# Weight forms cut in halves, bank copies with priority, single banks for the last two value products, and a later up unit, in a hybrid recurrent/retention block

## The chip, the cores and the metric

The kernel runs on one core of a Trainium2 chip. The core has five engines that work side by side, each through its own instructions in a fixed order: TensorE (PE, with its weight loads as PEld), VectorE (DVE), ScalarE (ACT), GpSimd (POOL) and SyncE (SP), beside 16 DMA engines. Matrix products land in PSUM, eight banks of 128 partitions by 2 KiB. An instruction that waits holds back all that stands behind it on its own engine. The metric is the device time of one execution in microseconds (us); the median of three runs before is 1076.57 us, from 1075.84 to 1076.70.

## The reference, cut to what matters

One block on 512 tokens (and 16 meta tokens ahead of them) of width 1024, all in f32:

```
z = rms_norm(h, norm_mix_g) @ w_in
u_rnn, u_gate, q, k, v, g_ret, ga, gb = split(z)
o_a = rg_lru(conv(u_rnn)) * gelu(u_gate)
o   = retention(rotary(q), rotary(k), v)          # 4 heads, 512 value columns each
o_b = head_rms(o) * silu(g_ret)
mixed = sigmoid(ga) * (o_a @ w_branch_rnn) + sigmoid(gb) * (o_b @ w_branch_ret)
h = h + mixed @ w_out
up = conv(rms_norm(h, norm_ffn_g) @ w_up);  gate, val = split(up)
h = h + (gelu(gate) * val) @ w_down
out = rms_norm(h, norm_final_g)[16:]
```

## The kernel before, in words

Every f32 operand of a product is cut into two fp16 forms: a high one, which ACT writes as a scaled copy (L91), and a low one, the rest, which DVE writes from the source and the high form (L92, `split`). A product is three matmuls (high by high, low by high, high by low). Weights come by DMA into tiles named `raw`, and their forms are written into tiles named `wt`, ten of them in a ring.

Twenty products of the middle of the kernel (the silu gate of retention, eight units; the two sigmoid gates, four and four; and the output of retention into the branch, four, of two weight units each) go by a scheme with seven products of half matrices in place of eight (`fast_products`, L835). Each of the seven is 12 matmuls of 257 columns for one weight unit. Its weight units (`fast_steps`, L234) are made in five steps: two cuts, a step `sums` with three additions on DVE (L253 to L255), two more cuts; a cut is a `split` of 128x512 or 128x1024. The seven products use three PSUM banks, `pa`, `pe` and `pb`. The first product (B11 by A11) goes into `pa` and ACT copies it to `kept` (L848, `keep`); the second (T3 by F7) goes into `pe`; the third (T2 by F6) is added onto `pa`, so it can't begin until that copy is done; it is copied to the other half of `kept`; the fourth goes into `pb`; the fifth (T1 by F5) is again added onto `pa` and copied to `last`; the sixth is added onto `pa` and the gate function `func` reads the bank (L881, names `g<-pa`); the seventh is added onto `pe`. Three DVE additions (L865, L869, L876) join copies and banks.

`gated(h)` (L983) runs the two gate units of a head, and between their products the retention output of the next head (`retention_out`, L928), which hands its tiles `or` on. `ob_forms` (L960) makes the forms `ob` of the gated output on DVE and ACT. `values(h)` (L883) computes the values of a head in five blocks of rows: four full ones (L906) and a small one (L898), each split into forms `v`. Up to here all five take space from PSUM tiles of two banks each (pool `acc`, two such tiles from head 2 on, beside four single banks in pool `bank`); blocks 0 and 1 share one tile, and 2 and 3 the other.

After the mix come the output projection of four row groups (L1179), each followed by an RMS norm: ACT squares and sums (L341) and takes the root (L343), DVE the reciprocal (L345) and the scaling into `xo` (L351), PE transposes (L358) and ACT and DVE split the result into `x2h` and `x2l`. While the last norm runs, PE works on three early half products of the up projection (L406), of which the third needs the second weight unit of `w_up`.

The order on every engine is not written out here: a scheduler places each instruction by the order of the code and by priorities, and `tc.high_priority()` raises one. `get(u)` makes the missing forms of a weight unit at its place in the code, and `tick()` makes one step of the next unit ahead of its use, as far as a bound on tiles allows (`ahead`).

Of the kernel before, what the change touches and what calls it, by code (L numbers as in the profile page):

```python
# [10 lines left out]
AF = mybir.ActivationFunctionType  # L11
ORDERED = {mybir.EngineType.PE, mybir.EngineType.Activation, mybir.EngineType.DVE}
ALU = mybir.AluOpType

P = 128
# [3 lines left out]
D = 1024  # L19
# [31 lines left out]
def hybrid_block_kernel(ctx, tc, x, meta, norm_mix_g, w_in, conv_w, conv_b, rg_a_w, rg_a_b,  # L51
# [21 lines left out]
    def acc(name):  # L73
        return psum["acc"].tile([P, 2, 512], F32, name=name, tag="acc")
# [15 lines left out]
    def split(hi, lo, src, s):  # L90
        nc.scalar.activation(hi, src, AF.Copy, scale=s)  # L91
        nc.vector.scalar_tensor_tensor(lo, src, s, hi, op0=ALU.mult, op1=ALU.subtract)  # L92
# [141 lines left out]
    def fast_steps(rv, bk, bc):  # L234


        tiles = []
        top, low = slice(0, bk), slice(bk, 2 * bk)
        left, right = slice(0, bc), slice(bc, 2 * bc)

        def cut(rows, cols):
            def run():
                t = wsp.tile([P, 2, 1024], F16, name="wt")
                src = rv[:, rows, cols]
                n = bk * src.shape[2]
                tv = [t[:, a, :n].rearrange("p (k c) -> p k c", k=bk) for a in range(2)]
                tiles.append(tv)
                split(tv[0], tv[1], src, SW)
            return run

        def sums():
            pair = rv[:, top].rearrange("p k (h c) -> p h k c", h=2)
            nc.vector.tensor_tensor(pair, pair, rv[:, :, right].rearrange("p (h k) c -> p h k c", h=2), op=ALU.add)  # L253
            nc.vector.tensor_tensor(rv[:, low, right], rv[:, top, left], rv[:, low, right], op=ALU.add)
            nc.vector.tensor_tensor(rv[:, low, left], rv[:, low, left], rv[:, low, right], op=ALU.add)  # L255

        at = {"B11": (0, 0), "B21": (1, 0), "B22": (1, bc), "T1": (2, 0), "T3": (2, bc), "T4": (3, 0), "T2": (3, bc)}

        def form(nm, a, k):
            i, c0 = at[nm]  # L260
            return tiles[i][a][:, k, c0:c0 + bc]

        wviews.append(form)
        return [cut(top, left), cut(low, slice(0, 2 * bc)), sums,
                cut(top, slice(0, 2 * bc)), cut(low, slice(0, 2 * bc))]
# [19 lines left out]
    def get(u):  # L285
        current[0] = max(current[0], u)
        while len(loaded) <= u:
            queue(unit_load())
        while done[0] < len(steps) and steps[done[0]][0] <= u:
            emit_step()  # L290
        return wviews[u]
# [46 lines left out]
    def rms_scale(src, rows, name):  # L338
        junk = work.tile([P, D], F16, name="junk", tag="w")
        ss = small.tile([P, 1], F32, name="ss")  # L340
        nc.scalar.activation(junk[:rows], src, AF.Square, accum_out=ss[:rows])  # L341
        sd = small.tile([P, 1], F32, name="sd")
        nc.scalar.activation(sd[:rows], ss[:rows], AF.Sqrt, scale=1.0 / D, bias=eps_t[:rows])  # L343
        rs = small.tile([P, 1], F32, name="rs")
        nc.vector.reciprocal(rs[:rows], sd[:rows])  # L345
        return rs

    def norm_rows(src, rows, g_bc, xn):
        rs = rms_scale(src, rows, "n")
        for a in range(2):  # L350
            nc.vector.scalar_tensor_tensor(xn[a][:rows], src[:, a * 512:(a + 1) * 512], rs[:rows], g_bc[a][:rows],  # L351
                                           op0=ALU.mult, op1=ALU.mult)

    def norm_transpose(rows, xhd, xld, s, xn):
        for a in range(2):
# [479 lines left out]
    def fast_products(ws, src, func, finish):  # L835


        last_k = 4 * len(ws) - 1

        def product(ps, wf, xf_, first=False):  # L840
            for k in range(last_k + 1):
                for aw, ax in SPLIT:
                    nc.tensor.matmul(ps[:, :257], ws[k // 4](wf, aw, k % 4), src(xf_, ax, k),  # L843
                                     start=first and k == 0 and (aw, ax) == (0, 0), stop=k == last_k and aw == 1,
                                     skip_group_check=True)

        def keep(dst, ps):
            nc.scalar.activation(dst, ps[:, :257], AF.Copy)  # L848

        kept, last = wtile("kept"), wtile("last")  # L850
        g0, g1 = wtile("g0"), wtile("g1")
        h0, h1 = slice(0, 257), slice(257, TQ)
        pa = bank("pa")
        product(pa, "B11", "A11", True)
        keep(kept[:, h0], pa)
        yield
        pe = bank("pe")
        product(pe, "T3", "F7", True)
        yield
        product(pa, "T2", "F6")  # L860
        keep(kept[:, h1], pa)
        yield
        pb = bank("pb")
        product(pb, "B21", "A12", True)
        nc.vector.tensor_tensor(g0[:, h0], pb[:, :257], kept[:, h0], op=ALU.add)  # L865
        yield
        product(pa, "T1", "F5")
        keep(last[:, h0], pa)
        nc.vector.tensor_tensor(g1[:, h1], pe[:, :257], last[:, h0], op=ALU.add)  # L869
        yield  # L870
        product(pa, "B22", "F3")
        func(g1[:, h0], pa[:, :257], -1.0, 0)
        func(g1[:, h1], g1[:, h1], -1.0, 257)
        finish(1, g1)
        product(pe, "T4", "A22")
        nc.vector.tensor_tensor(g0[:, h1], pe[:, :257], kept[:, h1], op=ALU.add)  # L876
        func(g0[:, :TQ], g0[:, :TQ], 1.0, 0)
        finish(0, g0)

# [3 lines left out]
    def values(h):  # L883
        vt = []
        wa, wb = get(u_v[h][0]), get(u_v[h][1])
        for b, (j0, nb) in enumerate(JB):
            if b % 2 == 0:
                ps = acc("ps")
            pb = ps[:, b % 2]
            vt.append(piece([P, 2, 512], F16, f"v{h}"))  # L890
            i = 0
            if b == 4:
                for r, wr in enumerate((wa, wb)):
                    for a in range(2):
                        for g in range(4):
                            m = 2 * NM if a == 0 else NM
                            xs = xlast[:, 4 * r + g].rearrange("p a t -> p (a t)")
                            nc.tensor.matmul(pb[32 * g:32 * g + m], xs[:, :m], wr(a, g, 0, 512),  # L898
                                             start=r == 0 and a == 0, stop=r == 1 and a == 1,
                                             tile_position=(0, 32 * g))  # L900
                split(vt[b][:, 0], vt[b][:, 1], pb, S_V / (SW * S_XN))
                continue
            for k in range(KD):
                w = wa if k < 4 else wb
                for ax, aw in SPLIT:
                    nc.tensor.matmul(pb, xf(ax, k, XF + j0, nb), w(aw, k % 4, 0, 512), start=i == 0, stop=i == 23)  # L906
                    i += 1
            split(vt[b][:, 0], vt[b][:, 1], pb, S_V / (SW * S_XN))
            tick()
        vv[h] = vt  # L910
# [257 lines left out]

    psum_layout(bank=2, acc=3)

    def out_proj(i):
        ps = acc("ps")
        halo = acc("ps") if i == 1 else None
        c0 = 2 + P * i
        ks = (0, 1, 2, 3, 4, 5, 7, 6) if i == 0 else range(KD)
        for k in ks:
            for n in range(2):
                for a, aw in SPLIT:
                    nc.tensor.matmul(ps[:, n], mx[k][:, a, c0:c0 + P], wo[k // 2](aw, k % 2, n * 512, 512),  # L1179
                                     start=k == 0 and (a, aw) == (0, 0), stop=k == ks[-1] and a == 1)  # L1180
                if halo is not None:
                    halo_part(halo, k, 4 * n)
        hv = h2[i].rearrange("p (a b) -> p a b", a=2)
        nc.vector.scalar_tensor_tensor(hv, ps, 1.0 / (SW * S_MX), hv, op0=ALU.mult, op1=ALU.add)
        xn = pair("xo")
        with tc.high_priority():
            norm_rows(h2[i], P, gffn, xn)
        return xn, halo

    def out_norm(i, xn):  # L1190
# [4 lines left out]
    for i in range(1, 4):  # L1195
        xn, halo = out_proj(i)
        xns.append(xn)
        if i == 1:
            halo_sum(halo)
        out_norm(i - 1, xns[i - 1])  # L1200
        tick()
        if i == 2:
            halo_finish()

# [5 lines left out]

    early = {}
    for ch, (u, col) in enumerate(((u_up[0][0], 0), (u_up[0][0], P), (u_up[0][1], 0))):
        wv = get(u)
        early[ch if ch < 2 else KF] = ps = acc("ps")
        mm = project_half(ps, wv, col, x2f, HU, 0)
        if ch == 1:
            with tc.high_priority(), tc.issue_after(mm):
                out_norm(3, xns[3])
# [252 lines left out]
```

## Time and profile before

| what | before |
|---|---|
| median of three runs | 1076.57 us |
| the profiled execution: its own time | 1075.74 us |
| its span, first to last instruction | 1073.5 us |
| PE busy | 1055.3 us, 98% |
| DVE busy | 839.3 us, 78% |
| ACT busy | 570.6 us, 53% |
| mean granted TensorE clock | 0.998 |

The profiled execution took 1075.74 us, 2.2 us more than its span, and 0.83 us less than the median. Times of single instructions are from the start of the span. A row of the timeline tells in square brackets how long the engine stood idle before the row and what ended that. The busy share of PE is its matmuls; a matmul's record is longer than the step to the next one, so short losses hide in a busy PE.

### The profile page before, as it was taken

Reading aid. Unit: us, or ns where it says so; the run is one execution under the profiler, and the core shown is the slowest. Engines: PE = TensorE matmul, PEld = TensorE weight load, DVE = VectorE, ACT = ScalarE, POOL = GpSimd, SP = SyncE. Lnnn points to the kernel's source line nnn. Section 1 sums busy time; section 2 is a strip of 40 time slices with the busy share of each in tenths; the row PEclk is TensorE's granted clock in tenths of the full one; section 3 lists DMA queues with packets and bytes.
Section 4 is the critical chain, followed back from the end, with each engine's and each line's share of the span. In section 5 each row is a group of like instructions: output and inputs, shape, how many; then the busy total and the mean of one; then the engine's idle time right before and its main releaser. Section 6 shows DMA issues by size and latency. Waiting matters only on the chain.

```text
span 1073.5 us, 21017 instructions
## 1 busy us (share of the span) xinstructions
PE 1055.3 (98%) x9043; PEld 856.1 (80%) x9043; DVE 839.3 (78%) x1242; ACT 570.6 (53%) x871; POOL 6.9 (1%) x20
## 2 busy tenths in 40 slices
PE   8999999999999999999999999999999999999997
PEld 6888888865684758888888885588888888888884
DVE  6884799998786969878697775578767767888875
ACT  8558954434564747566454453365444544454442
POOL 2000000000000000000000000000000000000000
PEclk9999999999999999999999999999999999999999
DMA  8331243431212212423333364143232323114322
GB/s 253 108 129 41 80 138 118 160 118 40 80 41 79 89 55 65 128 89 119 103 104 118 118 208 167 45 153 118 79 118 79 119 80 118 41 60 129 108 80 78
DMA packets 108988, 111.48 MB, mean 104 GB/s; under 512 B 5610, under 2 KB 100560, under 8 KB 108896
## 3 DMA queue, kind: packets, MB, share of 16 engines
q1 hardware_dynamic: 108448, 109.74, 31.9%
q8 instruction: 70, 1.15, 0.4%
q10 hardware_dynamic: 160, 0.27, 0.1%
q0 software_dynamic: 288, 0.14, 0.1%
q14 instruction: 22, 0.18, 0.1%
HBM read 108.04 MB, written 2.10 MB: 103 GB/s over the span
## 4 chain that ended last, share of the span: by engine, by line
PE 77%; DVE 14%; ACT 7%; issue 1%; DMA 0%; ACTq 0%; DVEq 0%
PE ps L393 35%; PE P L1307 9%; PE pa L843 9%; PE ps L906 4%; PE pm L393 4%; PE ps L1179 4%; PE pe L843 4%; DVE wt L92 3%; PE ps L406 2%; PE pb L843 2%; ACT wt L91 2%; PE ps L928 1%; DVE rnn L640 1%; DVE raw L253 1%; DVE v L92 1%
## 5 line engine op out<-in xcount | busy, mean ns | idle before, releaser
L393 PEld LDWEIGHTS <-wt 128*128 128x128 f16 x4224 | 410.4, 97 | 63.8 <-DVE t L734 1.4
L92 DVE SCALAR_TENSOR_TENSOR wt<-raw,wt 128x1024 f16<-128x1024 f32 (+2 forms) x270 | 296.5, 1110 | 70.9 <-ACT wt L91 68.8
L91 ACT ACTIVATE wt<-raw 128x1024 f16<-128x1024 f32 (+2 forms) x270 | 256.6, 966 | 159.1 <-PE ps L393 28.2
L843 PEld LDWEIGHTS <-wt 128*128 128x128 f16 x2016 | 195.0, 97 | 36.0 <-issue 8.8
L393 PE MATMUL ps<-x2h,wt 128*128 128x258 f16 x1440 | 218.8, 273 | 0.0
L393 PE MATMUL ps<-xh,wt 128*128 128x257 f16 (+2 forms) x1056 | 163.8, 275 | 1.1 <-DVE t L734 1.1
L393 PE MATMUL ps<-x2l,wt 128*128 128x258 f16 x720 | 137.7, 272 | 0.0
L1264 DVE SCALAR_TENSOR_TENSOR cv<-ps,vt,cv 128x512 f32<-128x512 f32 x96 | 71.9, 749 | 54.8 <-ACT cv L1262 53.4
L393 PE MATMUL ps<-xl,wt 128*128 128x257 f16 (+2 forms) x528 | 102.2, 275 | 0.0
L1307 PE MATMUL P<-wt,act 128*128 128x256 f16 x792 | 88.3, 273 | 0.0
L1307 PEld LDWEIGHTS <-act 128*128 128x128 f16 x792 | 77.5, 98 | 9.0
L906 PE MATMUL ps<-wt,xh 128*128 128x512 f16 x256 | 76.4, 379 | 1.2 <-DVE v L92 1.0
L843 PE MATMUL pa<-xs,wt 128*128 128x257 f16 x576 | 71.6, 273 | 4.7 <-ACT kept L848 4.4
L1262 ACT ACTIVATE cv<-ps,vt,vt 128x512 f32<-128x512 f32 x48 | 37.1, 774 | 57.0 <-PE ps L393 52.5
L393 PE MATMUL pm<-oa,wt 128*128 128x257 f16 x480 | 55.4, 274 | 0.0
L906 PEld LDWEIGHTS <-xh 128*128 128x128 f16 x256 | 24.8, 98 | 30.9 <-issue 2.9
L906 PE MATMUL ps<-wt,xl 128*128 128x512 f16 x128 | 48.5, 379 | 0.0
L843 PE MATMUL pa<-ob,wt 128*128 128x257 f16 x384 | 45.7, 274 | 0.6 <-ACT last L848 0.5
L1179 PE MATMUL ps<-wt,mx 128*128 128x512 f16 x192 | 44.3, 378 | 0.0
L253 DVE TENSOR_TENSOR raw<-raw 128x1024 f32<-128x1024 f32 x35 | 42.7, 1220 | 0.6
L1179 PEld LDWEIGHTS <-mx 128*128 128x128 f16 x192 | 17.6, 98 | 18.5
L928 PE MATMUL ps<-sc,v 128*128 128x257 f16 (+4 forms) x384 | 32.1, 236 | 0.0
(264 smaller groups left out, 1279.0 us busy)
## 6 DMA issues: line engine op xcount, KB each, us to landing
raw<-in_w_in SPq DMA_DIRECT2D x40, 1024.0 KB, 5.0
raw<-in_w_up SPq DMA_DIRECT2D x24, 1024.0 KB, 5.3
raw<-in_w_down SPq DMA_DIRECT2D x48, 256.0 KB, 3.3
raw<-in_w_branch_ret SPq DMA_DIRECT2D x16, 512.0 KB, 4.7
raw<-in_w_branch_rnn SPq DMA_DIRECT2D x8, 640.0 KB, 4.4
raw<-in_w_out SPq DMA_DIRECT2D x4, 1024.0 KB, 5.1
xin<-in_x SPq DMA_DIRECT2D x4, 512.0 KB, 5.7
raw<-in_w_in SPq DMA_DIRECT2D x4, 512.0 KB, 8.4
```

What stands on the lines that cost most here:

```text
L91: nc.scalar.activation(hi, src, AF.Copy, scale=s)
L92: nc.vector.scalar_tensor_tensor(lo, src, s, hi, op0=ALU.mult, op1=ALU.subtract)
L253: nc.vector.tensor_tensor(pair, pair, rv[:, :, right].rearrange("p (h k) c -> p h k c", h=2), op=ALU.add)
L393: nc.tensor.matmul(ps[:, hf, :n], w(aw, k, col, P), src(ax, k, c0, n), start=k == 0 and (aw, ax) == (0, 0), stop=k == nk - 1 and aw == 1)
L406: mm = nc.tensor.matmul(ps[:, hf, :n], w(aw, k, col, P), src(ax, k, c0, n), start=k == 0 and (aw, ax) == (0, 0), stop=k == KD - 1 and aw == 1)
L843: nc.tensor.matmul(ps[:, :257], ws[k // 4](wf, aw, k % 4), src(xf_, ax, k), start=first and k == 0 and (aw, ax) == (0, 0), stop=k == last_ ...
L906: nc.tensor.matmul(pb, xf(ax, k, XF + j0, nb), w(aw, k % 4, 0, 512), start=i == 0, stop=i == 23)
L928: nc.tensor.matmul(ps[:, hf, s0 - lo_i:257], vt[b][:, va, d * P:(d + 1) * P], st[SCP[b][0]][:, sa, o:o + hi_i - s0], start=i == 0, stop=i ...
L1179: nc.tensor.matmul(ps[:, n], mx[k][:, a, c0:c0 + P], wo[k // 2](aw, k % 2, n * 512, 512), start=k == 0 and (a, aw) == (0, 0), stop=k == ks ...
L1262: nc.scalar.activation(vv_, ps[:, :, 2:258], AF.Identity, scale=vt2[:, 96 + ch:97 + ch], bias=b_ff[:, ch:ch + 1])
L1264: nc.vector.scalar_tensor_tensor(vv_, ps[:, :, j:j + 256], vt2[:, 48 * j + ch:48 * j + ch + 1], vv_, op0=ALU.mult, op1=ALU.add)
L1307: nc.tensor.matmul(pd[:, 256 * tt:256 * tt + 256], t[:, ax, c0 + tt * P:c0 + tt * P + P], w(wf, aw, i), start=q % 6 == 0 and tt == 0 and i ...
```

## The change

It has four parts. The numbers behind L are lines of the kernel before; after the change `keep` stands in L854, the new `add` in L858, the halved copy in L249, the root in L345 and the value products in L919 and L911.

1. In the weight units of the seven-product scheme, the ACT copy of a cut is issued in pieces of two k-rows: two copies of 128x512 in place of one of 128x1024, two of 128x256 in place of one of 128x512. The DVE instruction of the cut stays whole. Of 24 units with four cuts each that makes 96 more ACT instructions; units of `w_down` are as they were.
2. The copies to `kept` and `last`, and the three DVE additions, are issued with high priority.
3. In `values(2)` and `values(3)` every block takes a single bank from the pool that the products' banks come from.
4. The step of weight forms behind the last norm's transposes is skipped, and the forms of the second up unit are made behind the last norm's root on ACT and its last scaling on DVE.

```diff
@@ fast_steps: cut
-                split(tv[0], tv[1], src, SW)
+                for a in range(0, bk, 2):
+                    nc.scalar.activation(tv[0][:, a:a + 2], src[:, a:a + 2], AF.Copy, scale=SW)
+                nc.vector.scalar_tensor_tensor(tv[1], src, SW, tv[0], op0=ALU.mult, op1=ALU.subtract)
@@ rms_scale
-        nc.scalar.activation(sd[:rows], ss[:rows], AF.Sqrt, scale=1.0 / D, bias=eps_t[:rows])
+        root[0] = nc.scalar.activation(sd[:rows], ss[:rows], AF.Sqrt, scale=1.0 / D, bias=eps_t[:rows]).ins
@@ norm_rows
+        return root[0], rr.ins                      # rr: the second scaling into xn
@@ fast_products
         def keep(dst, ps):
-            nc.scalar.activation(dst, ps[:, :257], AF.Copy)
+            with tc.high_priority():
+                nc.scalar.activation(dst, ps[:, :257], AF.Copy)
+
+        def add(dst, ps, k):
+            with tc.high_priority():
+                nc.vector.tensor_tensor(dst, ps[:, :257], k, op=ALU.add)
-        nc.vector.tensor_tensor(g0[:, h0], pb[:, :257], kept[:, h0], op=ALU.add)
+        add(g0[:, h0], pb, kept[:, h0])
...
@@ values
-            if b % 2 == 0:
-                ps = acc("ps")
-            pb = ps[:, b % 2]
+            if h >= 2:
+                pb = bank("pv")
+            else:
+                if b % 2 == 0:
+                    ps = acc("ps")
+                pb = ps[:, b % 2]
@@ out_proj, the loop behind it, and the early halves
-            norm_rows(h2[i], P, gffn, xn)
+            behind[0] = norm_rows(h2[i], P, gffn, xn)
-        tick()
+        if i < 3:
+            tick()
-        wv = get(u)
+        if ch < 2:
+            wv = get(u)
+        else:
+            with tc.issue_after(behind[0][0]), tc.issue_after(behind[0][1]):
+                wv = get(u)
```

On ACT, in the second gate unit of `gated(1)`, around the copy of the first product (at 364 us in the trace before). `g` is a gate, `ob` the forms of the gated output, `wt<-raw` a weight form; before:

```order
L881 ACTIVATE g_4172<-g_4172 128x514
L91 ACTIVATE ob_4361<-or_3680 128x257
L91 ACTIVATE ob<-or_3681 128x514
L91 ACTIVATE wt<-raw 128x1024
L848 ACTIVATE kept<-pa 128x257
L91 ACTIVATE ob<-y 128x514
L91 ACTIVATE ob<-d 128x514
```

The same place after the change:

```order
L249 ACTIVATE wt<-raw 128x512
L891 ACTIVATE g_4186<-g_4186 128x514
L249 ACTIVATE wt<-raw 128x512
L91 ACTIVATE ob_4378<-or_3686 128x257
L91 ACTIVATE ob<-or_3687 128x514
L854 ACTIVATE kept<-pa 128x257
L91 ACTIVATE ob<-y 128x514
L91 ACTIVATE ob<-d 128x514
```

The whole weight form that stood between `ob` and the copy is gone from there, and the two halves of one form stand around the gate; the copy follows `ob` directly.

On PE, in `values(2)`, where block 1 begins (at 331 us in the trace before). `ps_4086` is the tile of blocks 2 and 3, `ps_4023` that of 0 and 1; in brackets what an instruction waits for; before:

```order
L906 MATMUL ps_4086<-wt_3927,xl_96 128x512
L906 LDWEIGHTS xh_95
L906 MATMUL ps_4086<-wt_3944,xh_95 128x512
L906 LDWEIGHTS xh_95
L906 MATMUL ps_4023<-wt_3861,xh_95 128x512 [waits DVE_49]
```

After, where block 1 (`pv_4065`) follows block 0 (`pv_4031`):

```order
L919 MATMUL pv_4031<-wt_3952,xh_95 128x512
L919 LDWEIGHTS xl_96
L919 MATMUL pv_4031<-wt_3952,xl_96 128x512
L919 LDWEIGHTS xh_95
L919 MATMUL pv_4065<-wt_3869,xh_95 128x512
```

Block 1 no longer stands behind the greater part of block 2, and its first matmul has no wait.

On ACT at the last norm (at 699 us in the trace before): `junk` is the squares, `sd` the root, `x2h` the forms of the transposed rows; before:

```order
L341 ACTIVATE junk,ss<-h_7821 128x1024
L91 ACTIVATE wt<-raw 128x1024
L343 ACTIVATE sd<-ss,eps_t 128x1
L91 ACTIVATE wt<-raw 128x1024 x3
L91 ACTIVATE x2h<-ptr 128x4x128 x2
```

After:

```order
L343 ACTIVATE junk,ss<-h_7921 128x1024
L345 ACTIVATE sd<-ss,eps_t 128x1
L91 ACTIVATE wt<-raw 128x1024 x4
L91 ACTIVATE x2h<-ptr 128x4x128 x2
L91 ACTIVATE wt<-raw 128x1024 x2
L1282 ACTIVATE cv<-ps,vt_93,vt_94 128x512
```

The root stands right behind the squares, with four weight forms behind it where three stood.

## Rows read from the trace of the kernel before

**Rows 1.** The page: busy time by engine, and one group's matmuls (mean ns, idle before)
```profile
PE 1055.3 (98%) x9043; PEld 856.1 (80%) x9043; DVE 839.3 (78%) x1242; ACT 570.6 (53%) x871; POOL 6.9 (1%) x20
...
L843 PE MATMUL pa<-xs,wt 128*128 128x257 f16 x576 | 71.6, 273 | 4.7 <-ACT kept L848 4.4
```
**Rows 2.** PE's waits: line waited for, us in total, times, longest
```profile
PE pa L843 <- ACT kept L848: 4.4, 8, 1.0
...
PE ps L906 <- DVE v L92: 1.0, 2, 0.5
...
PE ptr L358 <- DVE xo L351: 0.7, 1, 0.7
```
**Rows 3.** Two stretches: length, then busy PE, PEld, DVE, ACT, POOL, clock
```profile
404.00:434.00 30.00, 28.60 (x278) 24.92 (x277) 29.01 (x50) 20.66 (x38) 0.00 (x0) 1.00 0.30 93
434.00:485.00 51.00, 50.82 (x455) 44.29 (x453) 40.78 (x54) 29.59 (x45) 0.00 (x0) 1.00 0.33 101
```
**Rows 4.** Timeline in gated(1): start, us, engine, operation, [idle before and releaser]
```profile
357.76 0.39 ACT L881 ACTIVATE g<-pa 128x257 f32<-128x257 f32 x1
...
359.48 1.49 PE L843 MATMUL pe<-xs,wt 128*128 128x257 f16 x12
...
362.24 0.94 ACT L91 ACTIVATE ob<-or 128x257 f16<-128x257 f32 x2 [1.71 <-DVE or L954]
...
363.44 1.06 ACT L91 ACTIVATE wt<-raw 128x1024 f16<-128x1024 f32 x1 [0.26 <-DVE raw L253]
...
364.40 0.37 ACT L848 ACTIVATE kept<-pa 128x257 f32<-128x257 f32 x1
...
364.82 1.49 PE L843 MATMUL pa<-xs,wt 128*128 128x257 f16 x12 [0.99 <-ACT kept L848]
```
**Rows 5.** Timeline, the same wait in later units
```profile
414.45 1.49 PE L843 MATMUL pa<-xs,wt 128*128 128x257 f16 x12 [0.34 <-ACT kept L848]
...
431.20 0.49 PE L843 MATMUL pa<-xs,wt 128*128 128x257 f16 x3 [0.90 <-ACT kept L848]
...
546.48 0.71 PE L843 MATMUL pa<-xs,wt 128*128 128x257 f16 x5 [0.60 <-ACT kept L848]
...
596.73 1.06 ACT L91 ACTIVATE wt<-raw 128x1024 f16<-128x1024 f32 x1 [2.66 <-DVE raw L253]
...
598.11 0.71 PE L843 MATMUL pa<-xs,wt 128*128 128x257 f16 x5 [0.48 <-ACT kept L848]
```
**Rows 6.** Timeline in values(2)
```profile
329.84 0.68 DVE L92 SCALAR_TENSOR_TENSOR ob<-d,ob 128x514 f16<-128x514 f32 x1
...
330.45 0.68 DVE L92 SCALAR_TENSOR_TENSOR v<-ps,v 128x512 f16<-128x512 f32 x1
...
331.18 0.59 PE L906 MATMUL ps<-wt,xh 128*128 128x512 f16 x2 [0.48 <-DVE v L92]
...
337.65 0.28 PE L843 MATMUL pa<-xh,wt 128*128 128x257 f16 x1
...
337.93 1.02 PE L898 MATMUL ps<-wt,xlast 128*32 128x512 f16 x13
```
**Rows 7.** Timeline at the last norm
```profile
699.11 1.05 ACT L91 ACTIVATE wt<-raw 128x1024 f16<-128x1024 f32 x1
...
700.06 0.29 ACT L343 ACTIVATE sd<-ss,eps_t 128x1 f32<-128x1 f32 x1
...
701.41 1.21 DVE L92 SCALAR_TENSOR_TENSOR wt<-raw,wt 128x1024 f16<-128x1024 f32 x1
...
702.54 1.41 DVE L351 SCALAR_TENSOR_TENSOR xo<-h,rs,gffn 128x512 f32<-128x512 f32 x2
...
703.43 0.63 PE L358 MATMUL ptr<-ident,xo 128*128 128x128 f32 x4 [0.65 <-DVE xo L351]
```
**Rows 8.** ACT's weight copies by form: busy us, mean ns
```profile
L91 ACT ACTIVATE wt<-raw 128x1024 f16<-128x1024 f32 x211 | 219.8, 1052 | 130.7 <-PE P L1307 23.7 <-PE ps L393 22.6 <-DMA raw<-in_w_in 17.9
...
L91 ACT ACTIVATE wt<-raw 128x512 f16<-128x512 f32 x43 | 26.8, 634 | 16.1 <-PE ps L393 5.5 <-PE pa L843 5.2 <-PE pm L393 2.6
```

More of the change, by code (lines that the diff above doesn't have):

```diff
@@ L346, in rms_scale @@
         return rs
+    root = [None]
     def norm_rows(src, rows, g_bc, xn):
@@ L350, in norm_rows @@
         for a in range(2):
-            nc.vector.scalar_tensor_tensor(xn[a][:rows], src[:, a * 512:(a + 1) * 512], rs[:rows], g_bc[a][:rows],
-                                           op0=ALU.mult, op1=ALU.mult)
+            rr = nc.vector.scalar_tensor_tensor(xn[a][:rows], src[:, a * 512:(a + 1) * 512], rs[:rows], g_bc[a][:rows],
+                                                op0=ALU.mult, op1=ALU.mult)
+        return root[0], rr.ins
     def norm_transpose(rows, xhd, xld, s, xn):
@@ L868, in fast_products @@
         keep(last[:, h0], pa)
-        nc.vector.tensor_tensor(g1[:, h1], pe[:, :257], last[:, h0], op=ALU.add)
+        add(g1[:, h1], pe, last[:, h0])
         yield
@@ L875, in fast_products @@
         product(pe, "T4", "A22")
-        nc.vector.tensor_tensor(g0[:, h1], pe[:, :257], kept[:, h1], op=ALU.add)
+        add(g0[:, h1], pe, kept[:, h1])
         func(g0[:, :TQ], g0[:, :TQ], 1.0, 0)
@@ L1169, in hybrid_block_kernel @@
     psum_layout(bank=2, acc=3)
+    behind = [None]
     def out_proj(i):
```

## The prediction

> **What bounds the kernel now.** I read the page first: PE is busy for 1055.3 us of the span of 1073.5, the other engines for 78% and 53% [rows 1]. The reader is to see there that less work on DVE or ACT would buy nothing by itself, and that this change can only win the little time in which PE stands still. So the second view is the list of PE's waits: three entries of it name something that the diff touches, the copies to `kept` (eight times, 4.4 us in all), the value forms `v` (twice, 1.0) and the scaled rows `xo` of the last norm (once, 0.7) [rows 2]. None of the list's entries is a weight form `wt`: forms come early enough everywhere, so making them faster is worth nothing, and making them later costs nothing up to their slack. Third came the timeline around each of these waits, and last the busy time by stretches, which says how full DVE is where work is moved.
>
> A wait costs more than its idle time. Twelve matmuls take 1.49 us [rows 4] while one lasts 0.27 [rows 1], so they start (1.49 - 0.27) / 11 = 0.11 us apart, and after a stop PE first waits out the end of the last one: idle of x costs x + 0.16. The entries are thus worth 4.4 + 8 x 0.16 = 5.7, 1.0 + 2 x 0.16 = 1.3 and 0.7 + 0.16 = 0.8 us.
>
> **Part 2 with part 1, the copies to `kept`.** At 364 us the first product had left its bank when PE began the second (359.48), yet the copy ran at 364.40 only: ACT waited for `or` from DVE, made two `ob` forms (to 363.2), waited for DVE again and made a whole weight form of 1.06 us, and the copy stood behind that; PE lost 0.99 + 0.16 [rows 4]. After the change the form is gone from that gap, but both `ob` forms, and with them the wait for DVE, still stand ahead of the copy. If `ob` came when it does now, the copy could begin near 363.1, PE at 363.5, and all would be won. Weight forms that moved ahead of `ob` delay it, though, so I take 0.6 of the 1.15. The later places [rows 5] go the same way: at 414 I take all of 0.50, since the copy is there only a little late; at 431 half of 1.06; at 546 half of 0.76, since a half form of 0.53 takes the place of a whole one of 0.95. At 598 the form that delays the copy runs for 1.06 us from 596.73; in the new order both its halves stand ahead of the copy, which makes that later by 0.1. Three of the eight are left, worth 5.7 - (1.15 + 0.50 + 1.06 + 0.76 + 0.64) = 1.6; by their places I take 0.7. Sum 0.6 + 0.5 + 0.5 + 0.4 - 0.1 + 0.7 = 2.6. The bounds are 4.4 (each loss down to its 0.16) and -0.9 (halves ahead of the copy in all eight, 0.11 each).
>
> The three additions move by a few places at most in DVE's order, since they stood nearly as early before; I cost that at nothing, between -0.5 and 0.3.
>
> **Part 1 by itself.** A copy of 128x1024 lasts 1.05 us, and the next engine step begins 0.95 after it began (699.11 to 700.06) [rows 7]: 0.10 overlap. A half lasts 0.63 [rows 8], so two halves hold ACT for 2 x 0.53 = 1.06, which is 0.11 more. 96 more instructions make 96 x 0.11 = 10.6 us of ACT. What hides it: ACT is idle for 47% of the span, and in the fullest stretch, 404 to 434 us, it is busy for 20.7 of 30 [rows 3]. DVE gets each form 0.11 later. It is the tight one there, 29.0 of 30 us, but has 10 us free in the 51 behind that [rows 3], so a delay is made up before a product misses a form. Price 0; if the cover went, 0.11 for each of the 16 cuts or so in that stretch, 1.8.
>
> The Trainium skill (VectorE: DVE Perf Modes, the section on the TRN2 errata for SBUF-source operations) speaks against the halves: a fixed cost is paid anew by each instruction, so tiles should have 512 elements or more; its table gives ScalarE 224 cycles at 1.2 GHz, 0.19 us an instruction as an estimate from that page. The rows above give 0.11, since neighbours overlap. By the page ACT would be held 18 us longer in place of 10.6, and at 598 the copy would be late by 0.2 in place of 0.1: the sum would fall by 0.1, and no run here shows more.
>
> **Part 3, the values.** In `values(2)` block 1 shares a tile with block 0, and its first matmul waits for DVE's split of block 0. That ran at 330.45 behind the `ob` forms of the last gate, so PE stood for 0.48, a loss of 0.64; the small block began 0.28 after the matmul before it where 0.11 is the step, a loss of 0.17 more, for the same reason one block on [rows 6]. `values(3)` repeats both, as the two entries of [rows 2] say. 2 x 0.81 = 1.6. With a single bank for each block, block 1 has no such wait. What is late next: blocks 2, 3 and 4 take the banks of earlier products and of block 0. A block is 24 matmuls of 512 columns, two of which last 0.59 [rows 6], some 5 us in all, so the split at 330.45, done at 331.1, is needed only when block 4 starts, past 340. I take 1.6. Below: if ACT and DVE held the banks up, one split of 0.68 a head, -0.5 net of what goes; above 2.1, if small gaps ahead of block 3 go too.
>
> **Part 4, the last norm.** The root ran at 700.06 behind a weight form, and DVE made another form (701.41) before it came to `xo` at 702.54; PE stood for 0.65, a loss of 0.81 [rows 7]. After the change the root follows the squares at once, 0.9 earlier, and no form stands between the reciprocal and `xo` on DVE: `xo` begins near 699.8 and its two halves of 0.71 are done by 701.3. PE reaches the transposes at 702.6. The loss goes: +0.8. In turn, four weight forms stand ahead of the `x2h` forms on ACT (4 x 0.95 from 699.6, to 703.4) and as many on DVE (4 x 1.21 from 701.3, to 706.1) ahead of `x2l`, which before was done at 706.2 or so. PE's third early half needs the same forms at 703.6 and 704.9, as they come, and the late `x2l` at about 706.4: a margin of nearly nothing. I take 0.8 with bounds 0.8 and -0.5. The raw weights behind that unit are asked for later by some ten us; no PE wait there names a DMA, and units behind it are first used more than 10 us later.
>
> **The sum.** 2.6 + 1.6 + 0.8 = 5.0, less 0.3 for new waits at the changed places that I can't see one by one: 4.7. Against the profiled execution's 1075.74 (a span of 1073.5 and 2.2 around it) that is 1071.0; the median of the runs stands 0.83 above that execution, so 1071.9, said as 1071.8.
>
> **Rivals.**
> A: the priority and the halves win nothing. For it: in the gated stage DVE is busy for 29.0 of 30 us [rows 3], so ACT's `ob`, ahead of the copy in both orders, comes when DVE comes to it, and PE merely stops somewhere else. Against: at 364 and 598 a whole weight form stands on ACT straight ahead of the copy [rows 4, 5], which is ACT's order and not DVE's pace. Then 1.6 + 0.8 = 2.4 is left: 1074.2.
> B: every loss goes but for the 0.16 at each: 4.4 + 2.1 + 0.8 = 7.3, so 1069.3. For it: nothing else waits in these places. Against: the copy still stands behind two forms at 598.
> C, slower: a copy or an addition with priority is placed so early that it stands at the head of its engine while PE still computes its bank, and holds back what was ready. The place is ACT ahead of `g<-pa`: that instruction frees the bank which the second product of the next unit takes. It was done at 357.76 + 0.39 = 358.15 and the product began at 359.48 [rows 4], so 1.33 us of delay cost nothing and each tenth beyond costs PE a tenth, in each of 20 units. At 0.4 beyond, 20 x 0.4 = 8.0 is lost against 4.7 won: 1079.9. It decides from 4.7 / 20 = 0.24 us a unit, that is from delays of 1.57. Against: around 364 the copy keeps its place behind `ob`, and nothing moved ahead of a bank's end there.
> D: it does not do what it says. Halves help only if the copy comes between them; where both stand ahead of it, as at 598, they are the whole form again. Were that so everywhere, the copies would cost 0.9: 1.6 + 0.8 - 0.9 = 1.5 gained, 1075.1.
>
> **Chances.** The forecast (2.5 to 7 us gained) 0.56, A 0.18, B 0.06, C 0.13, D 0.07. What a measurement of this kernel can tell from no change is 0.2%, 2.15 us, so faster means below 1074.4. The forecast and B are faster, and half of A: 0.71. The other half of A, all of D and 0.03 of C, where it just eats the gain, are the same: 0.19. The rest of C is slower: 0.10. The range holds A, B and D and leaves out most of C, and a gain above B's, together some 0.15: 1068.3 to 1076.5; the forecast's own range is 1069.6 to 1074.1.
>
> **What would show it.** Right: PE's waits on `v` and on `xo` leave the list, the entry for `kept` falls from 4.4 to about 2, ACT's busy time rises by some 10 us with 96 more instructions, and no `wt` enters the list. Wrong: an entry for a product behind `g<-pa` or for a bank (C), the same 4.4 spread over other units (A), `x2l` as a wait near 706 (part 4), or a `wt` near 430 (the cover of part 1).

## The result, and the profile after

The change makes the kernel slower. The median after is 1079.89 us (six runs, 1078.0 to 1082.0) against 1075.76 before (six runs, 1075.34 to 1076.7); the ratio is 1.0037, with a 95% interval from 1.0025 to 1.0048. The forecast was 1071.8, and its range ended at 1076.5. The profiled execution took 1080.57 us, of which 1078.5 is its span, 5.0 more than before.

| what | before | after |
|---|---|---|
| median | 1075.76 us | 1079.89 us |
| span of the profiled execution | 1073.5 us | 1078.5 us |
| ACT instructions counted as busy | 871 | 967 |
| PE's wait for `kept` | 4.4 us in 8 | 9.7 us in 9 |
| PE's waits for `v` of heads 2 and 3, and for `xo` | 1.0 and 0.7 us | none |

The page's line of busy times, to be held against [rows 1]:

```profile
PE 1056.0 (98%) x9043; PEld 856.7 (79%) x9043; DVE 838.3 (78%) x1242; ACT 578.3 (54%) x967; POOL 6.9 (1%) x20
```

The reader is to see that the work is the same to a microsecond on PE and DVE, and that ACT has the 96 instructions more and 7.7 us. Of the 5.0 us, PE's busy time takes 0.7; the other 4.3 are idle time of PE. PE's waits after (line waited for, us in total, times, longest), to be held against [rows 2]:

```profile
PE pa L848 <- ACT kept L854: 9.7, 9, 2.8
...
PE pa L848 <- ACT last L854: 0.9, 2, 0.5
```

The entries for `v` at L919 and for `xo` are gone, as forecast. But the copies, which were to be early, are later than before: PE waits up to 2.8 us for one, where 1.0 was the longest. The places are 362, 413 and 427 us, as before and by 0.1 to 0.9 worse, and three where before had no such wait: 463 (0.6), 493 (1.1) and 499 (2.8). Matched by number, the matmuls of PE start as early as before at 483 us and 5.9 us later at 500: nearly all of the loss falls in that stretch.

The last two places show the cause best. The timeline of the kernel after (start, us, engine, operation, idle before and its releaser):

```profile
490.56 0.74 ACT L91 ACTIVATE wt<-raw 128x640 f16<-128x640 f32 x1 [3.19 <-DMA raw<-in_w_branch_rnn]
...
492.93 0.37 ACT L854 ACTIVATE kept<-pa 128x257 f32<-128x257 f32 x1
...
493.35 1.49 PE L848 MATMUL pa<-xs,wt 128*128 128x257 f16 x12 [1.10 <-ACT kept L854]
...
495.52 1.24 ACT L249 ACTIVATE wt<-raw 128x256 f16<-128x256 f32 x3 [1.32 <-DMA raw<-in_w_in]
...
498.54 0.36 ACT L854 ACTIVATE kept<-pa 128x257 f32<-128x257 f32 x1
...
498.95 2.63 PE L848 MATMUL pa<-xs,wt 128*128 128x257 f16 x12 [2.79 <-ACT kept L854]
```

ACT stands at a weight form whose raw weights have not landed, and the bank copy stands behind it in ACT's order. PE then waits for the copy. At 499, ACT's wait of 1.32 us for the load explains as much of PE's 2.79 us at most; the rest is the work that stands between that form and the copy, late weight forms among it. The list of PE's waits names `kept`; only ACT's own rows name the DMA. ACT's waits for loads from 340 to 510 us, after:

```profile
ACT wt L249 <- DMA raw<-in_w_in: 7.7, 6, 2.1
ACT wt L91 <- DMA raw<-in_w_branch_rnn: 3.2, 1, 3.2
ACT wt L91 <- DMA raw<-in_w_in: 0.7, 1, 0.7
```

They are 11.6 us in all; the same list of the kernel before has none. The last row of the timeline has a second loss: twelve matmuls take 2.63 us where the row of 493.35 has 1.49. The stretches (length, busy PE, PEld, DVE, ACT, POOL, granted clock, DMA share, GB/s):

```profile
492.00:499.00 7.00, 3.11 (x28) 2.46 (x26) 4.29 (x8) 5.56 (x13) 0.00 (x0) 1.00 0.65 210
499.00:502.60 3.60, 3.60 (x19) 2.54 (x19) 3.60 (x9) 2.17 (x4) 0.00 (x0) 0.53 0.13 44
```

Behind this stretch with two stops of PE the granted clock is 0.53, the lower of its two levels (1.2 GHz in place of 2.4) but for the edges, for 3.6 us: 19 matmuls in 3.60 us, 0.19 apart in place of 0.11, some 1.5 us more.

The loads were late because they were asked for late. SP issues a load of raw weights when one of the two `raw` tiles is free, that is when the last form made from it is done. Four of these issues before:

```profile
444.62 0.37 SPq L102 DMA_DIRECT2D raw<-in_w_in  x1
...
461.89 0.37 SPq L102 DMA_DIRECT2D raw<-in_w_in  x1
...
477.50 0.37 SPq L102 DMA_DIRECT2D raw<-in_w_branch_rnn  x1
...
482.63 0.37 SPq L102 DMA_DIRECT2D raw<-in_w_in  x1
```

And the same four after:

```profile
455.25 0.37 SPq L102 DMA_DIRECT2D raw<-in_w_in  x1
...
472.42 0.37 SPq L102 DMA_DIRECT2D raw<-in_w_in  x1
...
486.22 0.37 SPq L102 DMA_DIRECT2D raw<-in_w_branch_rnn  x1
...
487.69 0.37 SPq L102 DMA_DIRECT2D raw<-in_w_in  x1
```

They are 10.6, 10.5, 8.7 and 5.1 us late, though PE is not late by then. The last two are those for which ACT waits at 490.56 and 495.52. They stand 1.5 us apart where before they stood 5.1, and the last is in use only 7.8 us after its issue, where these loads take a median of 5.0 us to land on the page of either kernel. Going back load by load, the first that is over 1 us late is the one at 344 us (by 3.0), right behind `values(2)`. This lateness is made up at 358 and 374 us (0.3 and 0.1). It comes back behind `values(3)`, 1.8 us at 395 and 5.2 at 412, and there it grows. Behind both, ACT makes its forms later than before; the rows are those of `values(2)`. ACT before, with the last of PE's rows on the small block of `values(2)`:

```profile
340.50 1.06 ACT L91 ACTIVATE wt<-raw 128x1024 f16<-128x1024 f32 x1 [2.27 <-PE ps L906]
...
341.80 1.06 ACT L91 ACTIVATE wt<-raw 128x1024 f16<-128x1024 f32 x1 [0.24 <-PE ps L906]
...
344.28 0.39 PE L898 MATMUL ps<-wt,xlast 128*16 128x512 f16 x3
...
345.36 1.06 ACT L91 ACTIVATE wt<-raw 128x1024 f16<-128x1024 f32 x1
```

The same after:

```profile
342.31 1.05 PE L911 MATMUL pv<-wt,xlast 128*32 128x512 f16 x16
...
342.42 0.60 ACT L91 ACTIVATE v<-pv 128x512 f16<-128x512 f32 x1 [4.58 <-PE pv L919]
342.96 1.15 ACT L249 ACTIVATE wt<-raw 128x512 f16<-128x512 f32 x2
...
344.50 1.14 ACT L249 ACTIVATE wt<-raw 128x512 f16<-128x512 f32 x2
345.54 0.37 ACT L854 ACTIVATE kept<-pa 128x257 f32<-128x257 f32 x1
```

Before, the form at 340.50 waits for PE: for the last full block to be done with one of the four weight tiles of this head, whose slot it takes. The small block reads all four tiles too, and before it had done 13 of its 16 matmuls at 337.93, ahead of block 3 [rows 6]. After, with a bank for each block, all 16 come last, from 342.31, so that no slot comes free until then, and the first form starts 2.5 us later. (Its row names no wait; it follows the copy to `v`, which waited for the block before.) At 345.4 ACT is still at its second form where before it began its third. That the small block's place causes this is theory S, and e5 to e7 below test it.

### The profile page after: what moved, and what is told of

Its sections match the earlier page's. It is cut to its first block, busy times and chain, and to the rows that moved or that the text cites. A ratio compares the mean times of both kernels' runs of the same rounds, so it can differ in the third digit from the quotient of the medians.

```text
span 1078.5 us, 21120 instructions
## 1 busy us (share of the span) xinstructions
PE 1056.0 (98%) x9043; PEld 856.7 (79%) x9043; DVE 838.3 (78%) x1242; ACT 578.3 (54%) x967; POOL 6.9 (1%) x20
## 4 chain that ended last, share of the span: by engine, by line
PE 76%; DVE 12%; ACT 7%; DMA 3%; issue 2%; ACTq 0%; DVEq 0%; SPq 0%
PE ps L398 34%; PE P L1327 9%; PE pa L848 8%; PE ps L1194 4%; PE pv L919 4%; PE pm L398 3%; PE pe L848 3%; PE ps L411 3%; DMA raw<-in_w_in 3%; PE ps L919 2%; DVE wt L250 2%; PE pb L848 2%; ACT wt L249 1%; PE ps L941 1%; DVE rnn L645 1%
## 5 line engine op out<-in xcount | busy, mean ns | idle before, releaser
L249 ACT ACTIVATE wt<-raw 128x512 f16<-128x512 f32 (+1 forms) x236 | 140.8, 639 | 107.7 <-PE P L1327 23.9
L250 DVE SCALAR_TENSOR_TENSOR wt<-raw,wt 128x1024 f16<-128x1024 f32 (+1 forms) x140 | 150.1, 1085 | 40.0 <-ACT wt L249 39.5
L92 DVE SCALAR_TENSOR_TENSOR wt<-raw,wt 128x1024 f16<-128x1024 f32 (+2 forms) x130 | 146.0, 1136 | 31.7 <-ACT wt L91 30.8
L91 ACT ACTIVATE wt<-raw 128x1024 f16<-128x1024 f32 (+2 forms) x130 | 125.3, 985 | 61.0 <-PE ps L398 19.4
L848 PE MATMUL pa<-xs,wt 128*128 128x257 f16 x576 | 72.7, 276 | 10.5 <-ACT kept L854 9.7
L919 PEld LDWEIGHTS <-xh 128*128 128x128 f16 x256 | 24.9, 98 | 29.1 <-issue 0.5
L919 PE MATMUL ps<-wt,xh 128*128 128x512 f16 x128 | 38.0, 379 | 0.1
L919 PE MATMUL pv<-wt,xh 128*128 128x512 f16 x128 | 38.0, 379 | 0.0
```

The costliest lines, as they stand in the source:

```text
L249: nc.scalar.activation(tv[0][:, a:a + 2], src[:, a:a + 2], AF.Copy, scale=SW)
L250: nc.vector.scalar_tensor_tensor(tv[1], src, SW, tv[0], op0=ALU.mult, op1=ALU.subtract)
```

## The experiments

The expectations number SP's loads in its order, from 0: load 42 is the one at 344 us before, and 51, 53, 55 and 56 are the four shown above. Theory L said that the forms, and with them the loads, are late because of part 3; rivals were P (the priority blocks ACT or DVE) and H (the halves cost more than they give). The first four runs undo one part, or two. All times are medians, of four runs for e11 and e12 and of eight to ten for the others. Beside them stand 29 runs of the kernel before at 1075.71 for e1 to e4, 29 at 1075.79 for e5 to e8 and 19 at 1075.71 for e9 to e12; the interval is that of the ratio to before, at 95%.

| run | parts | small block | us | ratio | interval |
|---|---|---|---|---|---|
| e1 | 3, 4 | last | 1078.81 | 1.0025 | 1.0014 to 1.0035 |
| e2 | 1, 2, 4 | as before | 1074.67 | 0.9991 | 0.9981 to 1.0000 |
| e3 | 1, 3, 4 | last | 1077.11 | 1.0018 | 1.0008 to 1.0027 |
| e4 | 2, 3, 4 | last | 1077.84 | 1.0024 | 1.0015 to 1.0034 |
| e5 | 1, 2, 3, 4 | fourth | 1073.14 | 0.9976 | 0.9966 to 0.9986 |
| e6 | 1, 3, 4 | fourth | 1073.87 | 0.9984 | 0.9975 to 0.9994 |
| e7 | 3, 4 | fourth | 1073.21 | 0.9976 | 0.9966 to 0.9985 |
| e8 | 4 | as before | 1075.31 | 0.9993 | 0.9983 to 1.0003 |
| e9 | 1, 2 | as before | 1075.02 | 0.9994 | 0.9984 to 1.0003 |
| e10 | 2, 3, 4 | fourth | 1072.61 | 0.9971 | 0.9962 to 0.9981 |
| e11 | 3, 4, and `ob` behind the copy | fourth | 1069.68 | 0.9944 | 0.9929 to 0.9959 |
| e12 | 2, 3, 4, and `ob` behind the copy | fourth | 1069.40 | 0.9941 | 0.9926 to 0.9956 |

**e1, parts 3 and 4 alone.** Against the changed kernel:

```diff
-                for a in range(0, bk, 2):
-                    nc.scalar.activation(tv[0][:, a:a + 2], src[:, a:a + 2], AF.Copy, scale=SW)
-                nc.vector.scalar_tensor_tensor(tv[1], src, SW, tv[0], op0=ALU.mult, op1=ALU.subtract)
+                split(tv[0], tv[1], src, SW)
...
-            with tc.high_priority():
-                nc.scalar.activation(dst, ps[:, :257], AF.Copy)
+            nc.scalar.activation(dst, ps[:, :257], AF.Copy)
```

> Parts 3 and 4 alone (single banks for the last values, later up unit); copies whole and without priority. Theory L (the weight forms are made later because of part 3, so their raw tiles come free later, loads are issued up to 10 us later, ACT waits for a load with the bank copy behind it near 490 to 500): the waits on v and xo go (-2.9 us), but loads 51 to 56 are late by 5 to 10 us and PE again waits for kept near 490 to 500, 3 us or more: 1075 to 1079. Theory P (priority of copies and additions is what costs): no late stretch, 1072.9. Theory H (halves cost): the same 1072.9.

It took 1078.81, slower than before without any half or priority, which refutes P and H as the whole cause. The load at 462 is 10.5 us late as with all parts, and ACT waits 10.2 us for loads from 340 to 510. PE's long wait, though, is one of 2.6 us for `last` at 491, where L had forecast 3 us or more for `kept`.

**e2, all but part 3.** Against the changed kernel:

```diff
-            if h >= 2:
-                pb = bank("pv")
-            else:
-                if b % 2 == 0:
-                    ps = acc("ps")
-                pb = ps[:, b % 2]
+            if b % 2 == 0:
+                ps = acc("ps")
+            pb = ps[:, b % 2]
```

> The change without part 3 (values in two-bank tiles as before). Theory L: loads 46 to 58 are issued within 1 us of before, no wait over 1.2 us near 490 to 500, clock 1.00 there; norm -0.8, copies -1 to -2.5: 1072.5 to 1074.5. Theory P or H: the long waits for kept near 490 to 500 stay, 1078 or more.

1074.67, just above L's range. Of the loads 46 to 58 all but one (3.6 late) are issued within 1 us of before, and PE has no wait for `kept` between 463 and 545. ACT waits 0.6 us for loads from 340 to 510. Part 3 is needed for the loss.

**e3, all but part 2.** Against the changed kernel:

```diff
-            with tc.high_priority():
-                nc.scalar.activation(dst, ps[:, :257], AF.Copy)
+            nc.scalar.activation(dst, ps[:, :257], AF.Copy)
...
-            with tc.high_priority():
-                nc.vector.tensor_tensor(dst, ps[:, :257], k, op=ALU.add)
+            nc.vector.tensor_tensor(dst, ps[:, :257], k, op=ALU.add)
```

> The change without part 2 (copies and additions at their old priority). Theory L: in the instruction order of this kernel the forms stand late by 7 us of DVE work at one place and by 2 behind it, in place of 11 with all parts, so the loads near 455 to 475 are late by a few us only and the stretch at 490 to 500 costs under 1 us: 1071.5 to 1074. Theory P: fast too, 1071.5 to 1074, so this run alone does not part L from P. Theory H: slow, 1078 or more.

1077.11: a miss for L's number and for the other two. I had read the delay off the instruction order, in DVE work, and that was too small. Three of the loads from 414 to 445 are late by 5 to 6 us, and those behind by 1 to 3; the same chain bites at another place. Timeline of e3:

```profile
455.60 0.72 ACT L249 ACTIVATE wt<-raw 128x256 f16<-128x256 f32 x2 [7.47 <-DMA raw<-in_w_in]
456.23 0.37 ACT L853 ACTIVATE last<-pa 128x257 f32<-128x257 f32 x1
...
456.65 0.60 PE L848 MATMUL pa<-xs,wt 128*128 128x257 f16 x4 [2.02 <-ACT last L853]
```

ACT stands for 7.47 us at a load, with the copy to `last` behind it. So where the late load hits depends on the rest of the order, and the mechanism is the same.

**e4, all but part 1.** Against the changed kernel:

```diff
-                for a in range(0, bk, 2):
-                    nc.scalar.activation(tv[0][:, a:a + 2], src[:, a:a + 2], AF.Copy, scale=SW)
-                nc.vector.scalar_tensor_tensor(tv[1], src, SW, tv[0], op0=ALU.mult, op1=ALU.subtract)
+                split(tv[0], tv[1], src, SW)
```

> The change without part 1 (whole copies in the cuts). Theory L: the forms stand late by 10 us of DVE work as with all parts, so the late loads and the waits near 490 to 500 stay: 1076 to 1080. Theory P: slow too, 1077 to 1080. Theory H: fast, 1071 to 1073.

1077.84, as L and P said and against H.

**e5, the small block fourth.** Theory S puts the lateness of part 3 down to the small block's place. Against the changed kernel:

```diff
-        for b, (j0, nb) in enumerate(JB):
+        turns = (0, 1, 2, 4, 3) if h >= 2 else range(5)
+        vt = [None] * 5
+        for b in turns:
+            j0, nb = JB[b]
...
-            vt.append(piece([P, 2, 512], F16, f"v{h}"))
+            vt[b] = piece([P, 2, 512], F16, f"v{h}")
```

> The whole change, but in values(2) and values(3) the small block is computed fourth and the last full block fifth. Theory S (in single banks the small block runs last and reads all four weight tiles to the end, so their slots come free 2.5 us later, the next forms and from there all loads are late): weight forms at 340 us begin within 1 us of the kernel before, loads 42 to 58 within 1.5 us, no wait over 1.2 us near 490 to 500, clock 1.00: 1072 to 1073.5. Rival R (single banks hold up the banks of the products, or the values' splits on DVE do): forms and loads stay late, 1077 or more.

1073.14: 6.75 us less than the changed kernel, from the order of two blocks that hold the same work. Loads 42 to 58 are 1 to 6 us earlier than before, more than S had said, and ACT's waits for loads from 340 to 510 fall from 11.6 to 2.0 us. ACT's forms in e5:

```profile
339.30 2.44 ACT L249 ACTIVATE wt<-raw 128x512 f16<-128x512 f32 x4 [0.79 <-PE pv L922]
```

Two whole forms, in four halves, are begun from 339.30, 3.7 us earlier than in the kernel after. S holds and rival R falls: single banks by themselves hold up nothing. The scheduler also places the instructions behind the two blocks anew; the runs do not part what the block's place does by itself from what the scheduler makes of it.

**e6, e7: the same without part 2, and without parts 1 and 2.** The edits are those of e3 and of e1, made in e5.

> As the run before, without part 2 (copies and additions at their old priority). Theory S: no late loads. What priority is worth is the difference to the run before: my forecast's term of 2.6 us for copies with halves would make this 1074.5; the run without part 3 suggests under 0.5 for both together, so 1072.5 to 1073.5.

> Parts 3 and 4 alone, with the small block fourth. Theory S: 1075.7 - 1.6 - 0.8 = 1073.3, all loads within 1 us of before. Rival R: like parts 3 and 4 with the small block last, 1078.8.

e6 took 1073.87, between the two numbers; e7 took 1073.21, 0.1 from S's 1073.3, though its loads are up to 5.6 us earlier than before and not within 1 us. Parts 1 and 2 together bring nothing that the runs can tell on top of parts 3 and 4: 1073.21 without, 1073.14 with.

**e8, part 4 alone.** Against the kernel before, the lines of the change in the norm, the loop behind it and the early halves.

> Part 4 alone. Both theories: the wait on xo goes, nothing else moves: 1075.7 - 0.8 = 1074.9. If the third early half then waits for its weight forms or x2l, 1075.5.

1075.31, between both, and its interval holds no change as well. The wait on `xo` is gone from the list and no other has come. In the trace of e8, PE is 0.10 us behind the trace of before ahead of the last transposes and 0.71 ahead of it at them, so the 0.8 is there. It then gives back 0.12 at 706.49, at a matmul that reads `x2l`, and 0.07 at 720, which leaves 0.6.

**e9, parts 1 and 2 alone.** Against the kernel before, the lines of the change in `cut`, `keep` and the three additions.

> Parts 1 and 2 alone. My forecast's term for the copies: -2.6, 1073.1. The runs so far: parts 1 and 2 together change the time by -0.6 where the values have two banks (1074.67 against 1075.31) and by -0.1 where they have one (1073.14 against 1073.21), so 1075.2 to 1075.7.

1075.02, 0.7 below before, and its interval reaches past 1. PE's waits in e9:

```profile
PE pa L845 <- ACT kept L851: 3.6, 6, 1.0
...
PE ps L913 <- DVE v L92: 1.2, 2, 0.6
...
PE ps L950 <- DVE v L92: 0.3, 1, 0.3
```

The entries for `kept` fall by 0.8 us and two places, where I had forecast some 2.4, and those for `v` grow by 0.5.

**e10, e5 without part 1.**

```diff
-                for a in range(0, bk, 2):
-                    nc.scalar.activation(tv[0][:, a:a + 2], src[:, a:a + 2], AF.Copy, scale=SW)
-                nc.vector.scalar_tensor_tensor(tv[1], src, SW, tv[0], op0=ALU.mult, op1=ALU.subtract)
+                split(tv[0], tv[1], src, SW)
```

> Parts 2, 3 and 4 with the small block fourth, weight copies whole. By the runs before, priority gives 0.7 (1073.87 to 1073.14, both with halves) and halves cost 0.7 (1073.21 to 1073.87, both without priority): 1072.5. If the two only work together (halves give priority a gap to use): 1073.2.

1072.61, near the 1072.5 of the simple sum. The differences between e5, e6, e7 and e10 are at most 1.3 us with overlapping intervals; that halves cost some 0.6 us and priority gives as much is likely, not shown.

**e11 and e12, the copy ahead of the `ob` forms.** Why did priority not move the copies? At 364 us they stand behind `ob` on ACT, which waits for DVE [rows 4], and they still do after. These runs move the `ob` forms of the first gate unit of `gated(h)` behind the first copy of the second. Against e7 (e11) and against e10 (e12):

```diff
+    copied = [None]
+    held = []
...
-            nc.scalar.activation(dst, ps[:, :257], AF.Copy)
+            copied[0] = nc.scalar.activation(dst, ps[:, :257], AF.Copy).ins
...
-            if j == 0:
+            if j == 0 and h < 3 and i == 0:
+                held.append(lambda: ob_forms(h, i, ot[2 * i], ot[2 * i + 1]))
+            elif j == 0:
                 ob_forms(h, i, ot[2 * i], ot[2 * i + 1])
...
+            if held:
+                with tc.issue_after(copied[0]):
+                    held.pop()()
```

> Parts 3 and 4 with the small block fourth, copies whole and without priority; in gated(h) the ob forms of the first gate unit are issued behind the first copy to kept of the second. If the copies wait because they stand behind ob in ACT's queue and ob waits for DVE: the three waits for kept near 313, 363 and 412 (0.95, 0.73 and 1.57 lost) go, 1073.2 - 2.7 = 1070.5. If the copies wait for something else (bank, DVE pace): waits move, 1072.5 to 1073.5.

> As the run before, with part 2 (priority). If priority works on copies apart from the ob forms as before: 0.7 less than the run before, near 1069.8. If what it gave was at the same three places, it adds nothing: same as the run before within 0.5.

e11 took 1069.68 and e12 1069.40, some 6 us less than before: the best kernels of this study. e11 is 3.5 us below e7. Its expectation took 2.7, the idle time of the three waits; with what PE loses beside it, as its own three numbers have it, they come to 3.25. The timeline of e11 at the place of [rows 4]:

```profile
357.50 0.63 ACT L887 ACTIVATE g<-g 128x514 f32<-128x514 f32 x1
358.03 0.37 ACT L854 ACTIVATE kept<-pa 128x257 f32<-128x257 f32 x1
...
358.73 1.49 PE L849 MATMUL pa<-xs,wt 128*128 128x257 f16 x12
...
359.83 0.94 ACT L91 ACTIVATE ob<-or 128x257 f16<-128x257 f32 x2 [1.43 <-DVE or L966]
```

The copy runs while the second product is computed, PE goes on without idle time, and the wait of 1.43 us for `or` stands behind the copy, where PE does not wait for it. PE's entry for the copies in e11:

```profile
PE pa L849 <- ACT kept L854: 2.1, 4, 0.8
```

The waits near 313, 363 and 412 are gone. With e12 within 0.3 of e11, priority adds nothing that the times can tell, though one more wait, of 0.6 us near 541, is gone from the trace of e12.

## Why the prediction was wrong

**Part 3 failed, at "what is late next".** I looked at who frees the banks, and at DVE's split, and those were right: the waits on `v` went, and no block waits for a bank. I did not look at what else the blocks hold. All five read the same four weight tiles, and the last one to read them decides when the next weight forms get their slots. Moving the blocks into single banks put the small block last. By the runs, part 3 with the small block fourth is worth 1073.21 - 1075.31 = -2.1 (e7 to e8), where I took a gain of 1.6; with the small block last it is 1078.81 - 1075.31 = +3.5 (e1 to e8). The place of the small block alone is thus worth 5.6 us without parts 1 and 2, and 1079.89 - 1073.14 = 6.75 with them.

**"Making them later costs nothing up to their slack" failed, too.** No product missed a form, that part held: no `wt` stands in PE's list. But a form does not only serve a product; it frees a raw tile, and that starts the next load. Late forms became loads up to 10.6 us late, the loads became ACT waiting at a form, and that became bank copies for which PE waits. I had priced the slack at the form's use and not at the load behind it, and left 0.3 us in the sum for new waits where 5.9 us came between 483 and 500. For the small delays of the halves alone the price of 0 held: in e9 ACT waits 0.6 us for loads from 340 to 510.

**Parts 1 and 2 were mis-sized: 0.7 in place of 2.6** (e9). Place by place in e9: 414 gained its 0.5 as forecast, 546 gave 0.33 of 0.4, 598 lost 0.05 of 0.1, but 364 gave 0.2 where I took 0.6, and 431 lost 0.1 where I took a gain of 0.5. By the steps between matmuls, waits for the copies cost PE 1.2 us less in e9 than before and those for `v` 0.6 more: 0.6 in all. The copies at 313, 364 and 431 stand behind `ob` in ACT's order, which neither halves nor priority changed. For the first copies of the second gate units e11 shows that this is the cause: with the order changed, the waits near 313, 363 and 412 go. No run moves the copy at 431, and e11 still has 0.8 us there, at 424.

**Part 4 was right in kind.** The wait on `xo` went and no entry for `x2l` came into the list; 0.8 was forecast, 0.5 measured (e8), and the trace of e8 has 0.6. The margin of nearly nothing at `x2l` is where 0.12 went.

**The halves cost ACT less than forecast:** 7.7 us more busy time for 10.6, or 0.08 for each added instruction in place of 0.11, and no PE wait in e9 names a form.

**The base.** The forecast added 0.83 us for the median of three runs before, 1076.57; six runs have 1075.76, so the forecast and its rivals stand 0.8 us too high from the start.

**The rivals.** C named 1079.9, a number that fits by luck, by a mechanism that does not: no PE wait names a bank held by `g<-pa`, and the loss is there without priority (e1). A, B and D, which all stay below the time before, fall with the forecast; of them A's claim, that the copies come no earlier, is nearest to what e5 and e7 show.

## What to carry to other kernels

When a change reorders the readers of a shared buffer, look at the last reader of every buffer that they hold, not only of the one that is changed, and follow each slot to the load that waits for it. A wait that the list puts down to a copy may be a DMA one step further back: read what the copy's own engine waited for. Where an instruction is late because it stands behind another that waits, raising its priority need not help; put the waiting one behind it.

## What was not expected of the hardware

The granted clock fell after some of the long idle times and not after others. In e1 PE stood for 2.57 us and went on at full clock:

```profile
491.49 0.71 PE L846 MATMUL pa<-xs,wt 128*128 128x257 f16 x5 [2.57 <-ACT last L851]
```

and the stretch behind it in e1:

```profile
491.60:506.00 14.40, 14.40 (x131) 12.62 (x130) 12.60 (x22) 10.89 (x18) 0.00 (x0) 1.00 0.36 115
```

In e4, after a longest wait of 3.2 us for `last`, the clock stood at half for 3.2 us:

```profile
490.80:494.00 3.20, 3.20 (x16) 2.24 (x16) 1.61 (x4) 2.90 (x5) 0.00 (x0) 0.50 0.69 212
```

So the lower clock cost some 1.5 us on top of the idle time in the kernel after (19 matmuls at 0.19 in place of 0.11) and about as much in e4 (16 at 0.20). The six runs of the kernel after spread over 4.0 us where the six of before spread over 1.4. The mean granted clock of each run points to the same cause: in e1 three runs have 0.999 and a mean span of 1075.7 us, and the five at 0.996 or 0.997 have 1077.2, 1.5 us more. A stretch of 3.6 us at 0.53 would lower the mean by 0.0016. Which stretch of a run was slow can't be told without its trace.
